# An encoder layer in fp32 on one core: Strassen steps in the down projections, a later attention step, a longer lag and earlier transposes

## The chip, the cores and the metric

The kernel runs on one core of a Trainium2 chip. The metric is device time in microseconds of that core. The times shown below are those of whole executions; the profile is of one further execution, with every instruction recorded. PE is TensorE, DVE is VectorE, ACT is ScalarE, POOL is GpSimd and SP is the queue that issues most loads.

## The reference

One layer over 256 tokens of width 2048, all in float32: a SwiGLU feed-forward block (FFN, inner width 5632) with half weight, two gated attention mixers side by side, and a second such FFN. Each part is framed by RMS norms.

```python
def swiglu(h, w_gate, w_up, w_down):
    return (jax.nn.silu(h @ w_gate) * (h @ w_up)) @ w_down

f = swiglu(rmsnorm(x, ffn1_pre_g), ffn1_w_gate, ffn1_w_up, ffn1_w_down)
x = x + 0.5 * rmsnorm(f, ffn1_post_g)
h = rmsnorm(x, mix_pre_g)
qa, ka, va, qb, kb, vb, ga, gb = jnp.split(h @ w_in, SPLITS, axis=-1)
...   # rope on q and k; sigmoid of ga, gb with a bias
out_a = windowed_gqa_sink(qa, ka, va, sink_logit)       # 8 heads on 2, |i-j| <= 128
out_b = differential_attention(qb, kb, vb, lam, ...)    # 4 heads, two softmaxes each
merged = ga * (out_a @ w_proj_a) + gb * (out_b @ w_proj_b)
x = x + rmsnorm(merged @ w_out, mix_post_g)
f = swiglu(rmsnorm(x, ffn2_pre_g), ffn2_w_gate, ffn2_w_up, ffn2_w_down)
x = x + 0.5 * rmsnorm(f, ffn2_post_g)
```

## The kernel before

**Products.** PE works in a rounded format, so every float32 operand is split in two: `hi`, a cast made by ACT (L178), and `lo`, the rest, a subtraction made by DVE (L180). A product of two operands is three matmuls: hi with hi, lo with hi, hi with lo (`mm3`, L201 to L203; `mm3s`, L259 to L261). The left operand (activations, transposed) is the stationary one, 128 x 128; 512 columns of a weight stream past it. Weights come from memory as units of 1 MB into `raw` (4 buffers), and are split into tiles `w` (6 buffers, so three pairs). `weights(k)` (L196) starts the split of unit k + `LA` (2) when unit k is used.

**Blocks.** `run_block` (L227) makes 512 columns of an output for both halves `h` of the tokens (2 x 128) and can let the second half lag by `lag` steps behind the first. `run_wide` (L263) makes 1024 columns: four results of 128 x 512, each in its own PSUM bank of eight. It walks over steps of 256 rows. A plain step ("N") is 24 matmuls. A step of kind "S" is one level of Strassen's method (seven products in place of eight, 21 matmuls): the weight unit gets three additions in place (L189 to L191) and a second pair of split tiles from the pool `big`; the left operand gets four sums and differences, made once by `make_forms` (L390, two steps share one `big` tile). The seven products have banks of their own, and after the last S step eight DVE operations and an ACT copy (L294 to L307) bring them together, after which plain steps go on in the same banks. `SKIND` gives the kinds of the eight steps of a gate or up block.

**An FFN** (`ffn`, L471) goes over eleven column blocks of the inner width in three parts, `PARTS`. Column block 0 is made alone, the others in pairs, first the gate block and then the up block of a pair. `up_after` multiplies, and defers the transposing of the result (`later`, L492) by a number of pumps; `pump` (L211) is called once a step. The transposed tiles `hT` (pool `big`, 9 tiles) are the left operand of the part's down blocks: two wide ones in parts one and two, whose results are added up in memory, and one wide and two narrow ones in part three, which end in the norm (`finish_f`) and the update of x (`post_norm`). All the down blocks' steps are plain.

**Seams.** Between FFN 1 and the mixer, and between the mixer and FFN 2, the last narrow block runs with `LAG`, and so does the first block after it. `make_xT` (L337) updates x (`upd`, L423), transposes it (L352) and writes the hi half on ACT (L358) and the lo half on DVE (L360) for each step of the first block. `tc.high_priority(HP)` moves what it holds ahead of 300 places in the order.

**Attention** runs between the steps of other blocks: `pipeline` (L816) is called by `pump` and at each tick runs the stages of several items, each stage at its own offset. `ItemB` has four stages: scores and softmax, transposing, product with v and norm (L738 to L740), transposing of the result (L750 to L754).

**What sets the order.** Only data dependences are written down. A planner (`schedule_with_timeline_sim=True`, L929) simulates the engines, gives out buffers and banks, and takes on each engine what is ready, by place in the program and priority. The order it finds is fixed in the program; on the chip every engine works through its own list.

Of the kernel before, what the change touches and what calls it, by code (L numbers as in the profile page):

```python
# [13 lines left out]
AF = mybir.ActivationFunctionType  # L14
ALU = mybir.AluOpType
# [10 lines left out]
NC = 512  # L26
# [3 lines left out]
NEG = -1e30  # L30
OFF_QA, OFF_KV, OFF_QB, OFF_KB, OFF_VB, OFF_GA, OFF_GB = 0, 1024, 1536, 2560, 3584, 4608, 6656
KU = D // (2 * P)
LAG = 2
LAG_END = 3
LA = 2
SKIND = "NSNSNSNN"
FIRST = (0, 2, 1, 4, 3, 6, 5, 7)
HP = 300
AHEAD = 2
# [5 lines left out]
def encoder_layer(  # L45
# [45 lines left out]
    def f32(ap):  # L91
        return ap.bitcast(F32)
# [50 lines left out]
    def queued(ins):  # L143
        return nullcontext() if ins is None else tc.issue_after(ins.ins)
# [63 lines left out]
    def later(fn, n=1):  # L208
        deferred.append([n, fn])
# [127 lines left out]
    def make_xT(gi):  # L337
        done = set()

        def pre(u, h):  # L340
            if (u, h) in done:
                return
            if not done:
                lo_of.clear()
            done.add((u, h))
            if h in upd:
                with queued(lo_of.get((u - AHEAD, h))):
                    upd[h](u)
            tp = tp_tile()
            for j in range(2):  # L350
                k = 2 * u + j
                nc.tensor.transpose(tp[:, j, :], x_sb[h][:, k * P:(k + 1) * P], ident)  # L352
            if h == 0:
                xT[u] = xTp.tile([P, 2, 2, SEQ], F32R, tag="xT", name=nm("xT"))
            t = xT[u][:, :, :, h * P:(h + 1) * P]
            gs = [gT[:, 16 * gi + 2 * u + j:16 * gi + 2 * u + j + 1] for j in range(2)]
            for j in range(2):
                hi_of[h] = nc.scalar.activation(t[:, 0, j, :], tp[:, j, :], AF.Copy, scale=gs[j])  # L358
            for j in range(2):
                lo_of[h] = nc.vector.scalar_tensor_tensor(  # L360
                    t[:, 1, j, :], tp[:, j, :], gs[j], f32(t[:, 0, j, :]), ALU.mult, ALU.subtract)
            lo_of[(u, h)] = lo_of[h]
            if u == 0:
                pre_ss[h] = small(4, f"pns{h}")
            if u % 2:
                n = u // 2

                def sq():
                    with queued(hi_of[h]):
                        nc.scalar.activation(t2(), x_sb[h][:, n * NC:(n + 1) * NC], AF.Square,  # L370
                                             accum_out=pre_ss[h][:, n:n + 1])
                if n == 3:
                    sq()
                else:
                    later(sq, 1)
            if u == KU - 1:
                s1 = small(1, "pn1")
                nc.vector.reduce_sum(s1, pre_ss[h], axis=AX.X)
                r_pre[h] = rsqrt_of(s1, 1.0 / D, EPS, "pn")
        return pre  # L380
# [6 lines left out]

    xS = {}

    def make_forms(kinds):  # L390

        for n, u in enumerate(u for u, k in enumerate(kinds) if k == "S"):
            if n % 2 == 0:
                fb = big([2, 2, 4, P])
            xf, sf = t2().rearrange("p (j t) -> p j t", j=2), t2().rearrange("p (f t) -> p f t", f=4)
            nc.vector.tensor_tensor(xf, f32(xT[u][:, 0]), f32(xT[u][:, 1]), ALU.add)
            a11, a12, a21, a22 = xf[:, 0, 0:P], xf[:, 1, 0:P], xf[:, 0, P:2 * P], xf[:, 1, P:2 * P]
            nc.vector.tensor_tensor(sf[:, 0], a21, a22, ALU.subtract)
            nc.vector.tensor_tensor(sf[:, 1], sf[:, 0], a11, ALU.subtract)
            nc.vector.tensor_tensor(sf[:, 2], a11, a21, ALU.subtract)  # L400
            nc.vector.tensor_tensor(sf[:, 3], sf[:, 1], a12, ALU.add)
            xS[u] = fb[:, n % 2]
            nc.scalar.copy(xS[u][:, 0], sf)
            nc.vector.tensor_tensor(xS[u][:, 1], sf, f32(xS[u][:, 0]), ALU.subtract)

    def split_T(src, n, hi, lo):
        tp = tp_tile()
# [63 lines left out]
    def ffn(post_g, pre, plan, lag, final, tail, x_src):  # L471
        hT = {}
        f = [None, None]
        ss = [small(4, f"fss{h}") for h in range(2)]
        last_c = [c_hi - 1 for _, c_hi in PARTS]

        def gate_up(c0, run_gate, run_up):
            s = {}

            def gate_after(h, c, acc):  # L480
                s[h, c] = t2()
                nc.scalar.activation(s[h, c], acc, AF.Silu, scale=r_pre[h])  # L482

            def up_after(h, c, acc):
                hh = t2()
                nc.vector.scalar_tensor_tensor(hh, acc, r_pre[h], s[h, c], ALU.mult, ALU.mult)

                def tr():
                    if c0 + c not in hT:
                        hT[c0 + c] = big([2, 4, SEQ])  # L490
                    split_T4(hh, hT[c0 + c], h)
                later(tr, 2 if c0 + 1 in last_c or c0 == 0 else len(SKIND))  # L492
            run_gate(gate_after)
            run_up(up_after)

        for part, (c_lo, c_hi) in enumerate(PARTS):
            for c in range(c_lo, c_hi):
                if c == 0:
                    gate_up(0, lambda a: run_block(plan["gate"][0], KU, lhs_x, a, lag, pre),
                            lambda a: run_block(plan["up"][0], KU, lhs_x, a))  # L500
                    make_forms(SKIND)
                elif c % 2:
                    gate_up(c, lambda a: run_wide(plan["gate"][c], lhs_x, xS.get, a),
                            lambda a: run_wide(plan["up"][c], lhs_x, xS.get, a))
            xlast = part == len(PARTS) - 1

            def down_after(h, c, acc, n, gb):
                if not xlast:
                    t = t2()
                    nc.scalar.copy(t, acc)  # L510
                    nc.gpsimd.dma_start(f_dram[h][:, (n + c) * NC:(n + c + 1) * NC], t,
                                        accum_op=ALU.add if part else ALU.bypass)
                else:
                    finish_f(acc, f, gb[c], ss[h], h, n + c, True, 4.0 / D, 4.0 * EPS, final)
            if xlast:
                for h in range(2):
                    f[h] = big([D], F32)
                    nc.gpsimd.dma_start(f[h], f_dram[h])
            lhs = lhs_of(hT, 2 * c_lo)
            for n in (0, 2):  # L520
                if xlast and n == 2:
                    reload_x(x_src)
                    for i in range(2):
                        gb = [load_bc(post_g[0, (n + i) * NC:(n + i + 1) * NC])]
                        run_block(plan["down"][part, n + i], 2 * (c_hi - c_lo), lhs,
                                  lambda h, c, acc, i=i, gb=gb: down_after(h, c, acc, 2 + i, gb),
                                  (LAG_END if final else LAG) if i else 0, tail=tail if i else None)
                else:
                    gb = [load_bc(post_g[0, i * NC:(i + 1) * NC]) for i in range(2)] if xlast else None
                    run_wide(plan["down"][part, n], lhs, None, lambda h, c, acc: down_after(h, c, acc, n, gb))  # L530

    def plan_ffn(w_gate, w_up, w_down):
        pl = {"gate": {}, "up": {}, "down": {}}
        for part, (c_lo, c_hi) in enumerate(PARTS):
            for c in range(c_lo, c_hi):
                if c == 0:
                    pl["gate"][0] = add_tall(w_gate[0], 0, D, 0)
                    pl["up"][0] = add_tall(w_up[0], 0, D, 0)
                elif c % 2:
                    pl["gate"][c] = add_wide(w_gate[0], 0, D, c * NC, SKIND, FIRST if c == 1 else None)  # L540
                    pl["up"][c] = add_wide(w_up[0], 0, D, c * NC, SKIND)
            r0, rows = c_lo * NC, (c_hi - c_lo) * NC
            pl["down"][part, 0] = add_wide(w_down[0], r0, rows, 0)
            if part < len(PARTS) - 1:
                pl["down"][part, 2] = add_wide(w_down[0], r0, rows, 2 * NC)
            else:
                for n in (2, 3):
                    pl["down"][part, n] = add_tall(w_down[0], r0, rows, n * NC)
        return pl
# [278 lines left out]
                  None if s else pres[1])  # L828
    run_wide(pm["qb"], lhs_x, None, q_after(qbT))
    run_wide(pm["vb"], lhs_x, None, v_after)  # L830
    ticker[0] = pipeline([ItemB(s, h, hh) for s in range(2) for h in range(2) for hh in range(2)], (0, 1, 2, 3), 1)
    run_block(pm["kv"], KU, lhs_x, kv_after)

    gates = {}
# [98 lines left out]
```

## Time and profile before

| | |
|---|---|
| three runs | 2080.92 us median (2079.74 to 2083.31) |
| the profiled execution | 2079.09 us, its span 2077.3 us |
| PE, weight loads of PE | 98% and 81% of the span, 9193 each |
| DVE, ACT, POOL | 69%, 48%, 3% |
| granted clock of TensorE, mean | 0.994 of full speed |
| DMA | 416 MB, 200 GB/s over the span |

Busy times are those of instructions on the engine; matmuls overlap their successors, so their mean duration is longer than the distance between two of them. "idle before <-" names what ended the wait of the instruction. A stretch of the second view below is named by its start.

### The profile page before, as it was taken

The numbers are of one execution on the slowest core, as the hardware profiler recorded it, in microseconds if no ns is written. First come the engines' busy times: TensorE is split into PE (matmuls) and PEld (weight loads), VectorE is DVE, ScalarE is ACT, GpSimd is POOL, SyncE is SP. The second block draws the span as 40 slices with busy tenths as digits, with TensorE's granted clock in tenths as the row PEclk, the third lists the DMA queues.
The fourth block names the chain that finished last, engine by engine and source line by source line (L and its number), as shares of the span: only waits on it lengthen the run. The fifth ranks groups of instructions, "written<-read, shape, count | busy, mean of one in ns | idle before, by whom it ended". The sixth has DMA issues, their size and how long they took to land. (4 is left out here: it accounts for less than half of the span.)

```text
span 2077.3 us, 22878 instructions
## 1 busy us (share of the span) xinstructions
PE 2036.5 (98%) x9193; PEld 1675.9 (81%) x9193; DVE 1431.5 (69%) x1413; ACT 987.9 (48%) x956; POOL 55.9 (3%) x91
## 2 busy tenths in 40 slices
PE   9999999999999999998999999999999999999997
PEld 7888887888878878887888888788888788887786
DVE  6984798647986675675675555569658885588854
ACT  7554545445554453454464344456445444454442
POOL 1000000000000010000000000000000000000000
PEclk9999999999999999999999999999999999999999
DMA  8556555676558646554545556546575656756672
GB/s 296 183 207 218 184 202 183 223 218 188 198 187 313 207 168 203 183 172 142 192 153 182 194 201 238 198 173 202 191 246 175 223 199 192 220 178 218 233 251 86
DMA packets 140570, 416.36 MB, mean 200 GB/s; under 512 B 8414, under 2 KB 9232, under 8 KB 139184
## 3 DMA queue, kind: packets, MB, share of 16 engines
q1 hardware_dynamic: 133872, 391.15, 54.7%
q0 software_dynamic: 6560, 23.75, 4.2%
q8 instruction: 72, 1.18, 0.2%
q14 instruction: 34, 0.28, 0.0%
q10 hardware_dynamic: 32, 0.01, 0.0%
HBM read 400.19 MB, written 14.68 MB: 200 GB/s over the span
## 5 line engine op out<-in xcount | busy, mean ns | idle before, releaser
L180 DVE TENSOR_TENSOR w<-raw,w 128x2048 fp32r<-128x2048 f32 (+3 forms) x376 | 796.5, 2123 | 492.5 <-ACT w L178 458.7
L178 ACT CAST w<-raw 128x2048 fp32r<-128x2048 f32 (+3 forms) x376 | 667.6, 1782 | 782.7 <-PE acc L260 607.7
L259 PE MATMUL acc<-w,xT 128*128 128x512 f32 x1368 | 536.0, 393 | 1.3 <-DVE acc L295 1.2
L260 PE MATMUL acc<-w,xT 128*128 128x512 f32 x1368 | 534.0, 390 | 0.0
L261 PE MATMUL acc<-w,xT 128*128 128x512 f32 x1368 | 513.0, 390 | 0.0
L259 PE MATMUL acc<-w,big 128*128 128x512 f32 x828 | 322.8, 390 | 1.1 <-ACT w L178 1.1
L260 PE MATMUL acc<-w,big 128*128 128x512 f32 x828 | 323.4, 391 | 0.0
L261 PE MATMUL acc<-w,big 128*128 128x512 f32 x828 | 318.0, 390 | 0.4 <-DVE w L180 0.4
L259 PEld LDWEIGHTS acc<-w,xT 128*128 128x128 f32 x1368 | 257.3, 188 | 57.6 <-DVE acc L295 3.0
L261 PEld LDWEIGHTS acc<-w,xT 128*128 128x128 f32 x1368 | 257.2, 188 | 53.3
L260 PEld LDWEIGHTS acc<-w,xT 128*128 128x128 f32 x1368 | 257.4, 188 | 51.7
L259 PEld LDWEIGHTS acc<-w,big 128*128 128x128 f32 x828 | 155.4, 188 | 34.0 <-ACT w L178 1.9
L261 PEld LDWEIGHTS acc<-w,big 128*128 128x128 f32 x828 | 155.5, 188 | 33.8 <-DVE w L180 2.0
L260 PEld LDWEIGHTS acc<-w,big 128*128 128x128 f32 x828 | 155.5, 188 | 31.7
L178 ACT CAST big<-raw 128x2048 fp32r<-128x2048 f32 (+1 forms) x64 | 118.9, 1860 | 89.2 <-DVE raw L191 85.4
L180 DVE TENSOR_TENSOR big<-raw,big 128x2048 fp32r<-128x2048 f32 (+1 forms) x64 | 141.5, 2219 | 23.0 <-ACT big L178 18.0
L202 PE MATMUL acc<-w,xT 128*128 128x512 f32 x208 | 82.5, 399 | 3.0 <-DVE xT L360 3.0
L201 PE MATMUL acc<-w,xT 128*128 128x512 f32 x208 | 82.0, 397 | 0.0
L203 PE MATMUL acc<-w,xT 128*128 128x512 f32 x208 | 79.3, 392 | 0.0
L201 PE MATMUL acc<-w,big 128*128 128x512 f32 x192 | 74.7, 389 | 0.0
L202 PE MATMUL acc<-w,big 128*128 128x512 f32 x192 | 74.7, 389 | 0.0
L203 PE MATMUL acc<-w,big 128*128 128x512 f32 x192 | 74.0, 389 | 0.0
(186 smaller groups left out, 1731.8 us busy)
## 6 DMA issues: line engine op xcount, KB each, us to landing
raw<-in_ffn_w_down SPq DMA_DIRECT2D x88, 1024.0 KB, 5.1
raw<-in_w_in SPq DMA_DIRECT2D x68, 1024.0 KB, 5.0
raw<-in_ffn_w_up SPq DMA_DIRECT2D x58, 1024.0 KB, 5.1
raw<-in_ffn_w_gate SPq DMA_DIRECT2D x57, 1024.0 KB, 5.2
raw<-in_ffn_w_gate SPq DMA_DIRECT2D x60, 512.0 KB, 4.7
raw<-in_ffn_w_up SPq DMA_DIRECT2D x60, 512.0 KB, 4.7
raw<-in_w_out SPq DMA_DIRECT2D x16, 1024.0 KB, 5.0
f_dram<-t POOLq DMA_DIRECT2D x32, 256.0 KB, 5.9
```

The source lines that it names most:

```text
L178: nc.scalar.copy(hi[:, sl], raw[:, sl])
L180: nc.vector.tensor_tensor(lo[:, sl], raw[:, sl], f32(hi[:, sl]), ALU.subtract)
L201: nc.tensor.matmul(o, lhi, rhi, start=first, stop=False)
L202: nc.tensor.matmul(o, llo, rhi, start=False, stop=False)
L203: nc.tensor.matmul(o, lhi, rlo, start=False, stop=last)
L259: nc.tensor.matmul(o, t[0], w[0][:, q, :], start=first, stop=False, skip_group_check=skip)
L260: nc.tensor.matmul(o, t[1], w[0][:, q, :], start=False, stop=False, skip_group_check=skip)
L261: nc.tensor.matmul(o, t[0], w[1][:, q, :], start=False, stop=last, skip_group_check=skip)
```

## The change

The down blocks of parts two and three that are made by `run_wide` get the kinds `DKIND`, with S at the second and the fourth of eight steps; the forms of their left operand are made after the gate block of the part's last pair, by a `make_forms` that takes any left operand. `LAG` goes from 2 to 3. The update of x and the two halves of x^T get priority. The transposes of an up block's first half of tokens are deferred by 2 pumps everywhere; those of the second half by 2 or 8 as before. The last stage of the differential attention's items runs one tick later.

```diff
-LAG = 2
+LAG = 3
 LAG_END = 3
 LA = 2
 SKIND = "NSNSNSNN"
+DKIND = "NSNSNNNN"
...
             if h in upd:
-                with queued(lo_of.get((u - AHEAD, h))):
+                with tc.high_priority(HP), queued(lo_of.get((u - AHEAD, h))):
                     upd[h](u)
...
-            for j in range(2):
-                hi_of[h] = nc.scalar.activation(t[:, 0, j, :], tp[:, j, :], AF.Copy, scale=gs[j])
-            for j in range(2):
-                lo_of[h] = nc.vector.scalar_tensor_tensor(
-                    t[:, 1, j, :], tp[:, j, :], gs[j], f32(t[:, 0, j, :]), ALU.mult, ALU.subtract)
+            with tc.high_priority(HP):
+                for j in range(2):
+                    hi_of[h] = nc.scalar.activation(t[:, 0, j, :], tp[:, j, :], AF.Copy, scale=gs[j])
+                for j in range(2):
+                    lo_of[h] = nc.vector.scalar_tensor_tensor(
+                        t[:, 1, j, :], tp[:, j, :], gs[j], f32(t[:, 0, j, :]), ALU.mult, ALU.subtract)
...
-    def make_forms(kinds):
+    def make_forms(kinds, lhs=None):
+        lhs = lhs or (lambda u: xT[u])
+        made = {}
...
+            v = lhs(u)
-            nc.vector.tensor_tensor(xf, f32(xT[u][:, 0]), f32(xT[u][:, 1]), ALU.add)
+            nc.vector.tensor_tensor(xf, f32(v[:, 0]), f32(v[:, 1]), ALU.add)
...
-            xS[u] = fb[:, n % 2]
-            nc.scalar.copy(xS[u][:, 0], sf)
-            nc.vector.tensor_tensor(xS[u][:, 1], sf, f32(xS[u][:, 0]), ALU.subtract)
+            m = made[u] = fb[:, n % 2]
+            nc.scalar.copy(m[:, 0], sf)
+            nc.vector.tensor_tensor(m[:, 1], sf, f32(m[:, 0]), ALU.subtract)
+        return made
...
-                later(tr, 2 if c0 + 1 in last_c or c0 == 0 else len(SKIND))
+                later(tr, 2 if h == 0 or c0 + 1 in last_c or c0 == 0 else len(SKIND))
...
         for part, (c_lo, c_hi) in enumerate(PARTS):
+            fS = {}
...
                 elif c % 2:
-                    gate_up(c, lambda a: run_wide(plan["gate"][c], lhs_x, xS.get, a),
-                            lambda a: run_wide(plan["up"][c], lhs_x, xS.get, a))
+                    off = 2 * c_lo
+                    def run_gate(a):
+                        run_wide(plan["gate"][c], lhs_x, xS.get, a)
+                        if c == c_hi - 2 and part:
+                            fS.update(make_forms(DKIND, lambda u: hT[(off + u) // 2][:, :, 2 * (u % 2):2 * (u % 2) + 2]))
+                    gate_up(c, run_gate, lambda a: run_wide(plan["up"][c], lhs_x, xS.get, a))
...
-                    run_wide(plan["down"][part, n], lhs, None, lambda h, c, acc: down_after(h, c, acc, n, gb))
+                    run_wide(plan["down"][part, n], lhs, fS.get, lambda h, c, acc: down_after(h, c, acc, n, gb))
...
-            pl["down"][part, 0] = add_wide(w_down[0], r0, rows, 0)
+            dk = DKIND if part else None
+            pl["down"][part, 0] = add_wide(w_down[0], r0, rows, 0, dk)
             if part < len(PARTS) - 1:
-                pl["down"][part, 2] = add_wide(w_down[0], r0, rows, 2 * NC)
+                pl["down"][part, 2] = add_wide(w_down[0], r0, rows, 2 * NC, dk)
...
-    ticker[0] = pipeline([ItemB(s, h, hh) for ...], (0, 1, 2, 3), 1)
+    ticker[0] = pipeline([ItemB(s, h, hh) for ...], (0, 1, 2, 4), 1)
```

## Rows read from the trace of the kernel before

**Rows 1.** The page, busy time, share of the span and instructions of each engine.
```profile
PE 2036.5 (98%) x9193; PEld 1675.9 (81%) x9193; DVE 1431.5 (69%) x1413; ACT 987.9 (48%) x956; POOL 55.9 (3%) x91
```

**Rows 2.** Stretches: length, each engine's busy time (instructions), clock, DMA share, GB/s.
```profile
293.90:340.00 46.10, 44.41 (x201) 35.84 (x200) 38.74 (x34) 23.37 (x19) 0.00 (x0) 1.00 0.54 183
340.00:381.80 41.80, 41.80 (x187) 34.61 (x186) 36.29 (x30) 21.41 (x15) 0.00 (x0) 1.00 0.58 201
381.80:426.90 45.10, 45.10 (x207) 37.34 (x206) 24.22 (x15) 20.55 (x16) 2.02 (x3) 1.00 0.57 190
426.90:470.40 43.50, 43.50 (x193) 36.02 (x192) 19.85 (x11) 17.12 (x12) 3.41 (x5) 1.00 0.74 219
470.40:512.70 42.30, 42.00 (x185) 34.23 (x185) 32.07 (x25) 20.38 (x15) 1.49 (x2) 1.00 0.75 219
...
710.20:735.70 25.50, 22.80 (x102) 18.26 (x100) 18.35 (x25) 11.92 (x16) 2.71 (x2) 1.00 0.69 236
735.70:766.10 30.40, 28.07 (x128) 22.14 (x129) 23.01 (x58) 17.99 (x50) 4.89 (x7) 0.94 0.41 144
...
903.30:965.00 61.70, 56.09 (x298) 48.01 (x297) 45.74 (x92) 35.50 (x78) 4.52 (x8) 0.97 0.45 149
965.00:1010.20 45.20, 45.20 (x195) 37.30 (x194) 18.37 (x13) 14.19 (x10) 0.00 (x0) 0.96 0.48 162
...
1315.50:1340.20 24.70, 22.44 (x102) 18.38 (x100) 15.24 (x21) 12.81 (x20) 0.64 (x2) 1.00 0.65 224
1340.20:1369.00 28.80, 27.64 (x125) 21.50 (x126) 20.26 (x51) 19.45 (x51) 3.25 (x6) 0.94 0.47 165
```

**Rows 3.** PE in order of time, near the start: start, us, operation.
```profile
17.75 1.47 PE L352 MATMUL tp<-ident,big 128*128 128x128 f32 x12
```

**Rows 4.** Waits of PE, whole span: total us, times, longest us.
```profile
PE tp L750 <- DVE t L740: 5.6, 1, 5.6
PE acc L259 <- ACT big L178: 3.5, 4, 0.9
...
PE acc L202 <- DVE xT L360: 3.0, 2, 2.1
PE tp L352 <- DVE big L423: 2.6, 1, 2.6
PE tp L409 <- ACT t L482: 2.6, 4, 0.7
PE acc L201 <- ACT xT L358: 2.3, 1, 2.3
```

**Rows 5.** DVE's groups by line and form: busy us, mean ns, idle before.
```profile
L180 DVE TENSOR_TENSOR w<-raw,w 128x2048 fp32r<-128x2048 f32 x290 | 663.4, 2288 | 413.3 <-ACT w L178 407.3 <-PE acc L260 5.2
L180 DVE TENSOR_TENSOR big<-raw,big 128x2048 fp32r<-128x2048 f32 x60 | 136.8, 2285 | 18.1 <-ACT big L178 18.0
L180 DVE TENSOR_TENSOR w<-raw,w 128x1536 fp32r<-128x1536 f32 x60 | 105.2, 1753 | 74.3 <-ACT w L178 46.6 <-issue 27.7
L189 DVE TENSOR_TENSOR raw<-raw 128x1024 f32<-128x1024 f32 x60 | 73.2, 1220 | 0.8
...
L190 DVE TENSOR_TENSOR raw<-raw 128x512 f32<-128x512 f32 x60 | 41.1, 686 | 0.5
...
L398 DVE TENSOR_TENSOR t<-t 128x128 f32<-128x128 f32 x6 | 1.7, 283 | 0.0
```

**Rows 6.** DVE in order of time, start of the up block.
```profile
342.52 1.76 DVE L180 TENSOR_TENSOR w<-raw,w 128x1536 fp32r<-128x1536 f32 x1 [6.92 <-issue]
```

**Rows 7.** DVE in order of time, end of the differential attention.
```profile
958.43 2.72 DVE L841 SCALAR_TENSOR_TENSOR t<-acc,pnr,t 128x512 f32<-128x512 f32 x4
961.07 2.28 DVE L180 TENSOR_TENSOR w<-raw,w 128x2048 fp32r<-128x2048 f32 x1
```

**Rows 8.** DVE in order of time, first block of the mixer.
```profile
758.86 2.28 DVE L180 TENSOR_TENSOR w<-raw,w 128x2048 fp32r<-128x2048 f32 x1
```

**Rows 9.** ACT in order of time, start of FFN 2.
```profile
1337.27 1.99 ACT L178 CAST w<-raw 128x1024 fp32r<-128x1024 f32 x2 [0.37 <-PE acc L202]
```

More of the change, by code (lines that the diff above doesn't have):

```diff
@@ L500, in ffn @@
                             lambda a: run_block(plan["up"][0], KU, lhs_x, a))
-                    make_forms(SKIND)
+                    xS.update(make_forms(SKIND))
                 elif c % 2:
-                    gate_up(c, lambda a: run_wide(plan["gate"][c], lhs_x, xS.get, a),
-                            lambda a: run_wide(plan["up"][c], lhs_x, xS.get, a))
+                    off = 2 * c_lo
[4 more added lines that the diff above has]
+                    gate_up(c, run_gate, lambda a: run_wide(plan["up"][c], lhs_x, xS.get, a))
             xlast = part == len(PARTS) - 1
@@ L830, in encoder_layer @@
     run_wide(pm["vb"], lhs_x, None, v_after)
-    ticker[0] = pipeline([ItemB(s, h, hh) for s in range(2) for h in range(2) for hh in range(2)], (0, 1, 2, 3), 1)
+    ticker[0] = pipeline([ItemB(s, h, hh) for s in range(2) for h in range(2) for hh in range(2)], (0, 1, 2, 4), 1)
     run_block(pm["kv"], KU, lhs_x, kv_after)
```

## The prediction

> **What bounds the kernel now.** I read the page's busy rows first, then the busy times by stretch, then TensorE's waits, then the instructions beside the largest waits.
>
> The busy row puts PE at 98% of a 2077.3 us span, DVE at 69%, ACT at 48% [rows 1]. The profiled execution took 2079.09 us, 1.8 us around the span; the median of the runs shown is 2080.92, so it lies 1.8 us under the median. A plain down block shows what PE does when nothing holds it: 192 products of 512 columns in 43.5 us (the two ends of the window add one record), 0.2266 us each (the stretch from 426.90) [rows 2]. The program has 8556 such products, 1939 us. The other 637 records of PE are transposes and short attention products; twelve transposes in a row take 1.47 [rows 3], 0.12 each, so these are 76 more. Some 62 us are not work: the start, the end and the waits below. Products that go away are therefore paid out nearly in full, and beside them only waits of PE can be won.
>
> The Trainium skill (Perfetto Trace Analysis, Identifying the Most-Contended Engine) says that matmul occupancy is a poor measure and that headroom is read from the busy share of LDWEIGHTS. By that the 81% here would mean a fifth to spare, and fewer products would bring little. The trace disagrees: in the down block at 426.90 PE waits for nothing and weight loads are still only 36.0 of 43.5 us, 83%. I keep the rule as a rival.
>
> PE's waits, with what each block took over its products (length less products times 0.2266, less 0.12 for each transpose):
> - last attention step: PE idle 5.6 us in one piece (L750) [rows 4], inside the block at 903.30; the clock is 0.97 there and 0.96 in the next block [rows 2]. At half clock (1.2 instead of 2.4 GHz) 0.04 x 45.2 = 1.8 us of the next block's work is lost.
> - end of FFN 1 and start of the mixer: 25.5 us for 96 products and 4 transposes, 3.3 over; 30.4 us for 96 and 32, 4.8 over (from 710.20 and 735.70) [rows 2]. In it 2.6 for L423, 2.1 (the longest of two) for L360 [rows 4], and the clock at 0.94, 0.06 x 30.4 = 1.8.
> - end of the mixer and start of FFN 2: 2.5 and 3.7 over (from 1315.50 and 1340.20) [rows 2]; 2.3 for L358, 0.9 (the rest of 3.0) for L360 [rows 4], the clock again 0.94, 1.7.
> - blocks such as 293.90, four times (gate of the second column pair of parts two and three): 46.1 - 41.5 - 16 x 0.12 = 2.7 each, where four deferred transposes fall at the gate block's end.
> - a wide S block after a plain down block (470.40, four times): 42.3 - 41.5 = 0.8. A wide up block (340.00) is 41.8 - 41.5 - 4 x 0.12, about 0.
>
> **The change, part by part.**
>
> *Strassen steps in six down blocks.* Two of eight row steps become 21 products instead of 24. Three wide blocks per FFN, two FFNs: 12 steps x 3 = 36 products fewer, 36 x 0.2266 = **-8.2 us**. All of them lie on PE, which sets the end.
>
> What it adds runs on DVE. A plain unit costs one 2.29 us subtraction; an S unit 1.75 + 1.22 + 2 x 0.69 + 2.29 = 6.64, so 4.35 more, 12 times 52 us [rows 5]. Closing a block adds eight operations of about 0.69, 5.5 us, six times 33. The forms of the left operand are per step 2 x 0.69 + 4 x 0.283 = 2.5, 5.0 per part, four times 20. Together 105 us on a DVE that has 646 idle: hidden as a sum, so the question is place.
> - Forms: DVE had 5.5 us free in the up block that takes them (36.3 of 41.8) and one hole of 6.9 just before its first weight split [rows 2, 6]. The last transposed halves of the previous pair are there by then, so I cost the forms at nothing. Without that cover they push up's splits back by up to 5.0 us, four times.
> - S phase: in a down block it is four steps, 90 products, 20.4 us, and the part's own transposes, 22.3 in the first block of a part. DVE must do two S units and two plain ones in it, 17.9; the first block also has 24.2 - 8 x 2.29 = 5.9 of evictions and transposes [rows 2, 5]. 23.8 against 22.3, less what starts early: nearly full. In the second block of a part 17.9 against 20.4 fits. No row shows an S phase in a down block. The bounds are 0 (340.00) and 2.7 (293.90) a block; I take 0.7, near the row that also follows a block boundary with a backlog (470.40): 6 x 0.7 = **+4.2**, ends 0 and +16.
> - Buffers: eight PSUM banks are full in that phase and the nine large buffers just suffice (four transposed tiles, two for x's forms or f, one for the new forms, one pair of weights), so the second S step's halves wait for the first step's products to let go. The plain step between (5.4 us) covers a 1.9 us cast and 2.29 subtraction. If not covered, it is in the 2.7.
> - Loads: the S units come as two halves instead of one, as the gate's already do, same bytes, DMA share 0.55 to 0.74 in these blocks [rows 2]. Nothing; a late one would add to the same stall.
>
> *Attention's last step one tick later.* Two transposes stand on PE for a chain (square, inverse root, scale) that sits on DVE behind four gate-bias operations, 2.72 us together, and a weight split of 2.28 [rows 7]. One tick is a plain step, 5.4 us of products that now stand ahead of the transposes. The wait goes to 0.2, and the lost clock with it: -(5.6 + 1.8) + 0.4 = **-7.0**. It moves two transposes, two ACT copies and two DVE subtractions, no DMA; their reader, the branch projection, comes after three more blocks. Late next is t2, a pool of eight: one more tile is alive (six of the item pipeline and two bias tiles). That is just eight; should it run over, a tick slips by about a step's wait, and 2 to 3 us come back. Ends: -7.4 and -3.
>
> *Lag 3 and priority at the two seams.* Lag 3 leaves six more products of the second half, 1.36 us, while the first half's norm runs. Priority puts the x update and the two halves of x^T ahead of weight splits. First seam: the 2.6 wait loses 1.36; the 2.1 wait goes, since a 2.28 split stood before L360 [rows 8]; of the 1.8 of clock I count half, as 1.2 of idle lies between the 0.9 that left the clock at 1.00 (293.90) and the 2.6 that did not. 1.4 + 2.1 + 0.9 = 4.4. Second seam: ACT ran a 1.99 us split pair ahead of L358 [rows 9]; with priority and 1.36 us of cover the 2.3 goes, with it the clock's 1.7 and the 0.9: 4.9. Sum **-9.3**. Cost: splits come later by the 0.6 to 1.1 us of what overtakes them, and with lag 3 three pairs of weights are alive of the six tiles, so in the tail block the fourth unit's split has one step, 2.7 us, for about 2.5. If it doesn't fit, 1 us a seam. The x writes on POOL's queue follow the update, not PE. Ends: -13 and -2.
>
> *Transposes of the first half after 2 pumps, not 8.* Eight of the 16 leave the end of four blocks where PE waited for L482 to free banks (2.6 in four) [rows 4], but their DVE and ACT work (1.3 us and 1.2) falls into the S phase of the gate block, whose last large cast was already 0.9 late [rows 4]. I take 0.75 off the 2.7: **-3.0**, ends -8 and +4.
>
> Sum: -8.2 + 4.2 - 7.0 - 9.3 - 3.0 = -23.3. Profiled 2079.1 - 23.3 = 2055.8; on the median 2080.9 - 23.3 = **2057.6 us**.
>
> **Rivals.**
> - *S phases fill DVE.* Each of the six costs the 2.7 of 293.90, not 0.7: +12.0, 2069.6. For: 23.8 against 22.3. Against: the second blocks fit. Chance 0.15.
> - *Everything moves well.* S phases cost nothing, both seams at their end, transposes gone: 2080.9 - 8.2 - 7.4 - 13 - 8, 2044. For: PE's order is re-planned around what is ready. Chance 0.07.
> - *The new plan keeps the waits.* The order comes from a simulated clock, which put the 5.6 us wait there in the first place; lag and priority only shift it. Strassen and half of attention remain: 2080.9 - 8.2 + 4.2 - 3.5 = 2073.4, up to 2080. Chance 0.10.
> - *The stream is not the bound.* The removed products turn into waits for splits (DVE 36.3 of 41.8 in up, 24.2 of 45.1 in down): 2057.6 + 8.2 = 2065.8. This is what the rule of the Trainium skill named above (Perfetto Trace Analysis) would give. The 43.5 us block without a wait speaks against. Chance 0.05.
> - *Slower: DVE bound at each part's last pair.* Forms land behind, not in, the 6.9 us hole: 4 x 5.0 = 20, the S phases that follow start late by as much and cost 2.7 each (16.2 instead of 4.2), and the seam's gains halve because splits are late there too: 2057.6 + 20 + 12.0 + 4.7 = 2094.3. It decides from the point where DVE has no hole over 1 us from the gate's end to the down block's fourth step. Chance 0.05.
>
> **How the numbers follow.** Forecast 0.58, its own range 2050 to 2066. The range for 8 in 10 takes in the full S phases and part of the plan that keeps its waits: 2046 to 2076. Within 0.2% (about 4 us, what a measurement of this kernel can tell) is 2076.8 to 2085.1. Faster: 0.57 + 0.14 + 0.07 + 0.04 + 0.05 = 0.87; same 0.07, mostly from the kept waits; slower 0.06.
>
> **What would show it.** 8520 products of 512 columns instead of 8556, at 0.2266. Down blocks with S of 186 products: right at 42.2 to 43 us without transposes, the S-phase rival at 45. The L750 wait gone and the clock at 1.00 through 1010. At the seams no wait for L360 over 0.5 us and at most one clock fall. The blocks like 293.90 at 45.3 us. The prediction is wrong if DVE has no hole before the up block's splits while PE waits for L178, L180 or L295 there, or if a wait of several us stands at a new place.

## The result, and the profile after

The changed kernel takes 2099.4 us (median of four runs, 2097.4 to 2101.35) beside 2081.43 for the kernel before on the same chip (2079.74 to 2083.31): a ratio of 1.0086, 95% interval 1.0073 to 1.0099. It is slower by 18 us where 23 less were forecast, and outside the range. The profiled execution took 2098.16 us, its span is 2096.4.

The busy row of the page after, to be read against [rows 1]: 36 fewer products, and PE, busy for about as long, fills less of a longer span. DVE has 144 more instructions and 96 us more work, where the prediction had counted 105.

```profile
PE 2034.7 (97%) x9157; PEld 1667.4 (80%) x9157; DVE 1527.3 (73%) x1557; ACT 1008.8 (48%) x982; POOL 55.8 (3%) x91
```

The same blocks by stretch, in the columns of [rows 2] (PE, PEld, DVE, ACT, POOL busy; clock; DMA share; GB/s):

```profile
295.70:341.00 45.30, 43.60 (x198) 35.58 (x197) 39.05 (x34) 22.79 (x19) 0.00 (x0) 1.00 0.53 186
341.00:385.80 44.80, 42.43 (x188) 34.49 (x187) 40.42 (x42) 22.45 (x17) 0.00 (x0) 1.00 0.54 188
385.80:433.40 47.60, 44.95 (x201) 35.88 (x200) 37.99 (x33) 22.07 (x17) 0.00 (x0) 1.00 0.46 159
433.40:477.20 43.80, 42.47 (x187) 34.76 (x186) 32.21 (x26) 21.77 (x18) 5.11 (x6) 1.00 0.76 231
...
720.80:745.60 24.80, 22.76 (x101) 18.21 (x99) 18.41 (x25) 11.87 (x16) 1.80 (x2) 0.99 0.77 263
745.60:777.20 31.60, 29.77 (x130) 23.23 (x130) 25.07 (x61) 18.15 (x50) 4.88 (x7) 0.90 0.37 134
914.30:970.00 55.70, 55.70 (x297) 47.40 (x295) 40.77 (x84) 29.93 (x67) 4.70 (x7) 1.00 0.47 159
970.00:1013.90 43.90, 43.90 (x198) 36.31 (x196) 23.30 (x22) 19.70 (x22) 0.55 (x1) 1.00 0.52 176
...
1343.90:1375.90 32.00, 27.89 (x125) 21.70 (x126) 20.75 (x51) 19.47 (x51) 3.25 (x6) 0.95 0.36 131
```

Beside [rows 2], with a removed product at 0.2266 us (six in a down block, 1.36):
- The up block that takes the forms: 44.8 for 41.8, +3.0. All four such blocks take 44.8; two of them had 43.2 before, so +9.2 for the four.
- The first down block of a part: 47.6 for 45.1 - 1.36, +3.9, four times: 15.5.
- The second: 43.8 for 43.5 - 1.36, +1.7, twice: 3.3.
- The last attention step and the block behind it: 55.7 for 61.7 and 43.9 for 45.2, the clock at 1.00 in both: -7.3.
- The first block of the mixer +1.2, with the clock at 0.90 for 0.94 (the last block of FFN 1 gives 0.7 back); the first of FFN 2 (1343.90) +3.2, with the clock at 0.95 for 0.94.

With -8.2 for the products, 2.3 in a gate block of FFN 2 behind a second down block, 1.3 at the start and -0.7 elsewhere this is 19.1, the difference of the two spans. The waits of PE after (total us, times, longest us):

```profile
PE acc L260 <- DVE acc L296: 14.1, 13, 1.4
PE acc L262 <- DVE big L181: 7.7, 8, 1.5
PE acc L260 <- ACT big L179: 6.0, 6, 2.3
PE acc L203 <- DVE xT L362: 4.3, 4, 1.8
...
PE acc L202 <- ACT xT L360: 3.9, 2, 2.3
PE acc L260 <- DVE acc L299: 3.8, 4, 0.9
```

(L179 and L181 are the cast and the subtraction of a split, before L178 and L180; L360 and L362 the halves of x^T, before L358 and L360; L296 to L308 the closing operations.) Beside [rows 4] the L750 wait is gone; the closings, L296 and L299, are the new head of the list. Of L296's 14.1, 8.0 lie in the six down blocks and 5.1 in the four gate blocks like 293.90, which waited for other things before. Three places show why.

**The up block.** DVE in order of time (start, us, operation, idle before and what ended it):

```profile
342.49 1.76 DVE L181 TENSOR_TENSOR w<-raw,w 128x1536 fp32r<-128x1536 f32 x1 [5.41 <-ACT w L179]
...
348.46 0.69 DVE L401 TENSOR_TENSOR t<-big 128x512 f32<-128x512 f32 x1
...
356.28 2.29 DVE L181 TENSOR_TENSOR big<-raw,big 128x2048 fp32r<-128x2048 f32 x1
...
369.30 0.70 DVE L409 TENSOR_TENSOR big<-t,big 128x512 fp32r<-128x512 f32 x1
```

and PE in the same block:

```profile
365.87 0.50 PE L260 MATMUL acc<-big,big 128*128 128x512 f32 x1 [0.90 <-ACT big L179]
...
369.45 0.96 PE L262 MATMUL acc<-big,big 128*128 128x512 f32 x3 [1.47 <-DVE big L181]
```

ACT at that time:

```profile
347.81 0.68 ACT L488 ACTIVATE t<-acc,pnr 128x512 f32<-128x512 f32 x1
```

The hole of [rows 6] is still there, 5.4 us, and empty. The forms (L401 to L409) come only after the last silu of the gate block (L488), from 348.46 on, between the splits of the Strassen units, which then reach PE 0.9 and 1.5 us late.

**The first down block.** DVE:

```profile
403.91 2.29 DVE L181 TENSOR_TENSOR w<-raw,w 128x2048 fp32r<-128x2048 f32 x1
406.12 0.69 DVE L296 TENSOR_TENSOR acc<-acc,t 128x512 f32<-128x512 f32 x1
406.72 2.28 DVE L181 TENSOR_TENSOR w<-raw,w 128x2048 fp32r<-128x2048 f32 x1
408.92 2.29 DVE L181 TENSOR_TENSOR big<-raw,big 128x2048 fp32r<-128x2048 f32 x1
411.12 2.29 DVE L181 TENSOR_TENSOR w<-raw,w 128x2048 fp32r<-128x2048 f32 x1
...
414.84 0.70 DVE L299 TENSOR_TENSOR acc<-acc,t 128x512 f32<-128x512 f32 x1
```

and what stopped PE:

```profile
406.87 0.50 PE L260 MATMUL acc<-w,big 128*128 128x512 f32 x1 [1.34 <-DVE acc L296]
413.46 0.50 PE L262 MATMUL acc<-w,big 128*128 128x512 f32 x1 [0.36 <-DVE w L181]
415.59 0.50 PE L260 MATMUL acc<-w,big 128*128 128x512 f32 x1 [0.94 <-DVE acc L299]
```

ACT in the same block:

```profile
404.26 1.91 ACT L179 CAST w<-raw 128x2048 fp32r<-128x2048 f32 x1
406.07 1.89 ACT L179 CAST big<-raw 128x2048 fp32r<-128x2048 f32 x1
```

DVE works from 386.9 to 418.0 with no gap over 0.3 us. At the first stop PE has made all products of the first four steps but twelve, those of the last Strassen unit's second pair (`big`). It waits for the first closing, L296, to go on with a later plain step; that closing stands behind the split of a later plain unit (403.91). The second pair is late in the same way: its cast (406.07) stands on ACT behind that of a later plain unit, its subtraction (408.92) on DVE behind two such splits. The twelve products therefore end only at 413, and then the next closings can run, up to the fourth (414.84), for which PE stops again. The three stops are 2.6 us of idle, and the restarts are slower. In the second down block PE stops once, 1.3 us, for an L296 that again stands behind one split; there DVE was idle for 2.1 us shortly before.

**The start of FFN 2.** ACT:

```profile
1340.97 1.99 ACT L179 CAST w<-raw 128x1024 fp32r<-128x1024 f32 x2 [1.80 <-PE acc L203]
...
1343.45 1.13 ACT L360 ACTIVATE xT<-tp,gT 128x128 fp32r<-128x128 f32 x4
...
1364.52 0.69 ACT L488 ACTIVATE t<-acc,pnr 128x512 f32<-128x512 f32 x1
...
1365.72 1.89 ACT L179 CAST w<-raw 128x2048 fp32r<-128x2048 f32 x1
1367.51 1.14 ACT L360 ACTIVATE xT<-tp,gT 128x128 fp32r<-128x128 f32 x4
```

The split pair of [rows 9] still stands ahead of the first hi half: the priority did not move it. With lag 3 the first half's silu (L488) and a split now also stand ahead of a later hi half, and PE waits once more.

### The profile page after: what moved, and what is told of

Same layout as the page of the kernel before. It is cut to its first block, busy times and chain, and to the rows that moved or that the text cites. A ratio compares the mean times of both kernels' runs of the same rounds, so it can differ in the third digit from the quotient of the medians.

```text
span 2096.4 us, 22995 instructions
## 1 busy us (share of the span) xinstructions
PE 2034.7 (97%) x9157; PEld 1667.4 (80%) x9157; DVE 1527.3 (73%) x1557; ACT 1008.8 (48%) x982; POOL 55.8 (3%) x91
## 5 line engine op out<-in xcount | busy, mean ns | idle before, releaser
L181 DVE TENSOR_TENSOR w<-raw,w 128x2048 fp32r<-128x2048 f32 (+3 forms) x376 | 789.4, 2108 | 417.0 <-ACT w L179 414.7
L179 ACT CAST w<-raw 128x2048 fp32r<-128x2048 f32 (+3 forms) x376 | 661.9, 1768 | 720.7 <-PE acc L261 564.5
L260 PE MATMUL acc<-w,big 128*128 128x512 f32 x768 | 300.5, 392 | 11.8 <-DVE acc L296 8.1
L261 PE MATMUL acc<-w,big 128*128 128x512 f32 x768 | 299.7, 390 | 0.0
L262 PE MATMUL acc<-w,big 128*128 128x512 f32 x768 | 290.6, 391 | 1.5 <-DVE w L181 1.5
L179 ACT CAST big<-raw 128x2048 fp32r<-128x2048 f32 (+1 forms) x76 | 141.6, 1865 | 99.3 <-DVE raw L192 95.3
L181 DVE TENSOR_TENSOR big<-raw,big 128x2048 fp32r<-128x2048 f32 (+1 forms) x76 | 169.1, 2232 | 25.8 <-ACT big L179 20.2
L260 PEld LDWEIGHTS acc<-w,big 128*128 128x128 f32 x768 | 144.2, 188 | 45.4 <-DVE acc L296 10.6
L262 PEld LDWEIGHTS acc<-w,big 128*128 128x128 f32 x768 | 143.9, 188 | 33.5 <-DVE w L181 3.9
L261 PEld LDWEIGHTS acc<-w,big 128*128 128x128 f32 x768 | 144.2, 188 | 29.3
L260 PE MATMUL acc<-big,big 128*128 128x512 f32 x228 | 89.7, 393 | 6.0 <-ACT big L179 6.0
L190 DVE TENSOR_TENSOR raw<-raw 128x1024 f32<-128x1024 f32 x72 | 88.1, 1223 | 1.4
L261 PE MATMUL acc<-big,big 128*128 128x512 f32 x228 | 88.9, 390 | 0.0
```

The source lines that it names most:

```text
L179: nc.scalar.copy(hi[:, sl], raw[:, sl])
L181: nc.vector.tensor_tensor(lo[:, sl], raw[:, sl], f32(hi[:, sl]), ALU.subtract)
L190: nc.vector.tensor_tensor(raw[:, 1::2], raw[:, 1:3], raw[:, 3:4].to_broadcast([P, 2, NC]), ALU.add)
L260: nc.tensor.matmul(o, t[0], w[0][:, q, :], start=first, stop=False, skip_group_check=skip)
L261: nc.tensor.matmul(o, t[1], w[0][:, q, :], start=False, stop=False, skip_group_check=skip)
L262: nc.tensor.matmul(o, t[0], w[1][:, q, :], start=False, stop=last, skip_group_check=skip)
```

## The experiments

The kernel before, with one part of the change each, comes first. Ratios are to the kernel before, timed beside each run on the same chip; its medians there are 2081.3 to 2082.6 us, so times of different runs compare to about 1 us.

**Attention alone.**

```diff
-(0, 1, 2, 3), 1)
+(0, 1, 2, 4), 1)
```

> The kernel before with the differential attention's last stage one tick later, nothing else. Theory A (the parts act where they stand, and the loss is in the Strassen steps and the seams): 7.3 us faster than before, 0.9965, PE's 5.6 us wait gone and no clock fall near 965. Theory B (the parts cost nothing alone; the planner's new order for all of them together makes the loss): also about 7 us faster, so this run checks the size only.

2073.39 us, ratio 0.9962 (0.9948 to 0.9977). The two blocks of [rows 2] at 903.30 and 965.00, the clock in the column after POOL's:

```profile
903.30:959.00 55.70, 55.70 (x296) 47.40 (x295) 40.90 (x84) 29.93 (x67) 4.71 (x7) 1.00 0.48 158
959.00:1003.00 44.00, 44.00 (x200) 36.45 (x199) 23.27 (x23) 19.98 (x21) 0.55 (x1) 1.00 0.53 179
```

The wait and its clock loss go with nothing in their place.

**Strassen with its forms alone** (the changed kernel with attention, transposes, lag and priority set back).

> The kernel before with the Strassen steps in the six down blocks and their forms, nothing else. Theory A: slower by about 20 us (8.2 less products; 9 more in the four up blocks that take the forms, 19 in the six down blocks), ratio 1.0096. Theory B: faster by some 4 to 8 us, since alone the S phases find the place they were given credit for.

2124.25 us, 1.0203 (1.0188 to 1.0218): 42 us slower, more than twice what the whole change loses: theory A in kind, at twice its size. By blocks: the down blocks lose what they lose in the changed kernel, but the four up blocks take 6.8 to 7.9 over their products instead of 2.9. So another part of the change softens the lateness of the forms there, most likely the early transposes; the runs don't separate it.

**The seams alone, then lag and priority apart.**

```diff
-LAG = 2
+LAG = 3
```

> The kernel before with lag 3 and the priority of the x update and of the halves of x^T, nothing else. Theory A: 3 to 5 us slower, with the wait for the first hi half still 2.4 us and a second wait of about 2 us late in FFN 2's first block. Theory B: faster by 5 to 9 us, as first forecast.

2086.7 us, 1.0026 (1.0015 to 1.0036), 4.7 slower: theory A.

> The kernel before with lag 3 alone. Theory L (the longer lag keeps a third pair of weights alive, the planner then plays the second half's products early, and the cover does not grow): the loss of the seams is the lag's, 4 to 6 us slower than before, ratio 1.002 to 1.003, the first wait for the hi half at FFN 2's start still 2.4 us. Theory H (priority is what hurts, by putting the splits behind): within 1 us of before.

2085.84 us, 1.0021 (1.0012 to 1.0031). The waits for x^T of the kernel with lag 3 alone:

```profile
PE acc L202 <- DVE xT L360: 3.9, 3, 1.8
PE acc L201 <- ACT xT L358: 3.9, 2, 2.3
```

Against [rows 4] (3.0 and 2.3) none got shorter by more than 0.3 and one more of each kind appeared; with the clock at 0.90 (0.94 before) the first block of FFN 2 is 4.5 longer. At the first seam the wait for L423 falls from 2.6 to 2.0.

> The kernel before with the priority of the x update and of the two halves of x^T alone. Theory L: the waits for L360 (2.1 and 0.9 us) go as forecast, 2 to 4 us faster. Theory H: 3 to 5 us slower.

2081.87 us, 1.0000 (0.9990 to 1.0010): neither theory. The planned order hardly differs from that of the kernel before: put side by side in order of time, 18 of 1413 DVE instructions and 12 of 956 on ACT are others than in the kernel before (by operation and tiles). The loss at the seams is the lag's.

**Transposes alone.**

```diff
-later(tr, 2 if c0 + 1 in last_c or c0 == 0 else len(SKIND))
+later(tr, 2 if h == 0 or c0 + 1 in last_c or c0 == 0 else len(SKIND))
```

> The kernel before with the transposes of the first half of tokens after 2 pumps everywhere, nothing else. Theory A: 1 to 3 us faster (the blocks of the second column pair lose 0.3 to 0.7 of their 2.7 each). Theory B: no change within 1 us.

2078.55 us, 0.9982 (0.9972 to 0.9991): 3.4 faster, a little more than theory A named. In the trace each pair of blocks like 293.90 and the up block ahead of it gains 0.4, the gate block from 46.1 to 45.3, the up block taking over four of its transposes: 1.7 for the four pairs. Another 0.6 and 1.0 are in the two last up blocks of part three.

**The changed kernel without its forms.** The Strassen steps of the down blocks use x's forms, which have the same size; the forms of their own left operand are left out.

> The changed kernel without making the forms of the down blocks' left operand; the S steps read x's forms instead, so the down products are of wrong operands while PE's work is the same. Theory F (the forms, 5 us of DVE, lie between the up block's weight splits): the four up blocks lose their 2.9 us of waits, 8 to 11 us faster than the changed kernel, about 2090. Theory G (the up blocks wait because large buffers or PSUM banks are short, not for DVE): no change within 2 us, 2098 to 2101.

2088.52 us, 1.0038 (1.0023 to 1.0053): 10.9 less than the changed kernel. The four up blocks fall by 3.0 each, to what [rows 2] shows at 340.00; the down blocks stay as they were (47.6, and 43.7 for 43.8). Of the 12 us, 3.4 come back in the gate and up block behind FFN 2's second down block. So the forms' lateness is the up blocks' loss, and not the down blocks'.

**The changed kernel without the three additions** on the Strassen units of the down blocks (their second operands are left as loaded).

> The changed kernel without the three additions on the weights of the down blocks' S units (2.6 us of DVE for each of 12 units; the second pair of tiles is then split from the plain weights, so the products are not the layer's). Theory C (the down blocks wait for the S unit's chain on DVE: split, additions, cast, split): the six down blocks lose 2.5 and 1.6 us, 11 to 15 us faster than the changed kernel, about 2086. Theory D (they wait for the closing operations, which stand behind weight splits however early the S unit is ready): 0 to 3 us faster.

2120.26 us, 1.0189 (1.0174 to 1.0204): both theories missed. With 12 x 2.6 = 31 us taken from DVE ([rows 5]; its busy time falls by 28.5) the kernel is 21 slower than the changed one. DVE in the first down block:

```profile
411.20 2.29 DVE L181 TENSOR_TENSOR big<-raw,big 128x2048 fp32r<-128x2048 f32 x1
417.23 0.69 DVE L298 TENSOR_TENSOR t<-acc,t 128x512 f32<-128x512 f32 x1 [3.75 <-PE acc L263]
```

DVE now has holes, and this block takes 11.3 over its products, 5 of them by a clock of 0.91; the other three first down blocks take 4.3 to 6.0 and the four up blocks 4.7 to 6.9. The planner found another order, with four transposes of each last pair moved into the down block. Only the second down blocks did as expected (1.7 to 0.3). The loss does not go by the amount of DVE work alone.

**Attention and transposes together.**

> The kernel before with the two parts that gained alone: attention's last stage a tick later, and the early transposes. If they add: 7.9 + 3.2 = 11 us faster than before, about 2071, ratio 0.9947. If the planner's new order for both undoes one: 2074 to 2078.

2071.03 us, 0.9942 (0.9925 to 0.9958): the two gains add up. This is the changed kernel's own gain with Strassen, lag and priority left out.

**Forms early.** The changed kernel with lag 2, without priority, and the forms made right behind the transposes that they need:

```diff
-                        if c == c_hi - 2 and part:
-                            fS.update(make_forms(DKIND, ...))
+                    if c == c_hi - 4 and part:
+                        later(lambda: fS.update(make_forms(DKIND, ...)), len(SKIND) - 1)
```

> The changed kernel with lag 2 and no priority, and with the forms asked for right behind the transposes they need, before the gate block's results take their buffers, so that DVE has them in its hole before the up block's splits. Theory F (the forms' place on DVE is what the up blocks pay for): the four up blocks lose 2.5 to 3 us each, the down blocks keep 4.1 and 1.7: 2099.4 - 4.5 for the lag - 11 = 2084. Theory M (it is the amount of DVE work around there, not the place): up blocks keep 2 us or more, about 2093.

2092.81 us, 1.0048 (1.0033 to 1.0063). The forms on DVE, first and last, and the up block:

```profile
333.86 0.68 DVE L401 TENSOR_TENSOR t<-big 128x512 f32<-128x512 f32 x1
...
340.03 1.29 DVE L409 TENSOR_TENSOR big<-t,big 128x512 fp32r<-128x512 f32 x2 [0.16 <-ACT big L408]
```

```profile
341.10:383.60 42.50, 42.16 (x188) 34.57 (x187) 37.16 (x31) 21.26 (x15) 0.00 (x0) 1.00 0.57 198
383.60:431.20 47.60, 44.92 (x201) 35.87 (x200) 37.99 (x33) 22.06 (x17) 0.00 (x0) 1.00 0.46 160
```

The hole can take them: 42.5 instead of 44.8, theory F by the blocks. The first down block keeps its 47.6, so its loss has another cause. The gain is not all kept, and so the time is the one that theory M named: the two gate blocks behind the second down blocks now take 3.0 and 4.2 over their products, 0.7 and 3.0 in the changed kernel, an up block behind them 2.3 more, and the seams give 3.2, not 4.5.

**Strassen steps third and sixth** instead of second and fourth, otherwise as the last one.

```diff
-add_wide(w_down[0], r0, rows, 0, dk)
+add_wide(w_down[0], r0, rows, 0, dk, (0, 2, 1, 4, 5, 3, 6, 7))
```

> As the run before, and the down blocks' two S steps stand third and sixth of eight with two plain steps between them, instead of second and fourth. Theory C (the S unit's chain on DVE, split, three additions, cast, split, and the plain unit's split behind it are late for PE since they start only when a weight pair comes free): the down blocks lose most of their 4.1 and 1.7 us, about 2084 - 15 = 2069, two us under attention and transposes alone. Theory D (the closing operations stand behind weight splits wherever the S steps are): the down blocks stay within 1 us of theirs, 2080 to 2086.

2088.77 us, 1.0027 (1.0018 to 1.0036). The second down blocks fall from 1.7 to 0.6 and 0.8, the first rise from 4.1 to between 5.8 and 6.9; but the granted clock is 0.93 in two of these and 0.97 in the other two, which is 3.5 and 1.5 us of their work, so without it they take 3.2 to 4.5. ACT there:

```profile
395.26 1.91 ACT L180 CAST w<-raw 128x2048 fp32r<-128x2048 f32 x1 [4.93 <-PE acc L262]
397.07 1.89 ACT L180 CAST big<-raw 128x2048 fp32r<-128x2048 f32 x1
```

The cast that PE waits for (2.2 us) stands behind one that itself waits 4.9 us for PE to free a pair of weight tiles. What made the first blocks dear was open still.

**Strassen steps fourth and sixth**, after three plain ones.

```diff
-add_wide(w_down[0], r0, rows, 0, dk, (0, 2, 1, 4, 5, 3, 6, 7))
+add_wide(w_down[0], r0, rows, 0, dk, (0, 2, 4, 1, 5, 3, 6, 7))
```

> As the kernel with the forms early (the changed kernel with LAG 2, no priority, forms behind the transposes), but the two Strassen steps of a down block are its fourth and sixth, after three plain steps (16 us). Theory B (the boundary: the first Strassen unit's splits meet the evictions and transposes that the up block leaves): the first down blocks fall from about 4 us over their products to 1.5 or less, four times, the second ones by 1 as with the third and sixth: 2092.8 - 10 - 2 = about 2081. Theory Q (the queue: a large cast stands on ACT behind a cast that waits for a free pair of weight tiles, wherever the Strassen step lies): the first down blocks keep 4 us or more and the time stays at 2089 to 2093.

2064.72 us (2061.85 to 2065.74), 0.9914 (0.9898 to 0.9931): theory B, and by more than it asked for. Its two down blocks of part two:

```profile
383.30:427.00 43.70, 43.70 (x201) 36.17 (x200) 35.10 (x30) 21.34 (x17) 1.15 (x2) 1.00 0.57 199
427.00:469.20 42.20, 42.20 (x187) 34.84 (x186) 31.60 (x24) 20.75 (x16) 3.47 (x5) 1.00 0.76 225
```

and DVE where the closing starts:

```profile
413.32 2.29 DVE L182 TENSOR_TENSOR w<-raw,w 128x2048 fp32r<-128x2048 f32 x1
415.53 0.69 DVE L297 TENSOR_TENSOR acc<-acc,t 128x512 f32<-128x512 f32 x1
```

PE is busy in all of both stretches. The first closing still follows a plain split, and so does the second pair's; but two more plain steps, 48 products or 10.9 us, now stand ahead of the last Strassen step. DVE has worked off what the boundary left (it is idle for 2.1 us before 408.78), and PE waits for nothing, if with little to spare: the closing at 415.53 ends as PE comes to need it. The two gate blocks behind take 2.2 and 3.5 less than with the forms early alone. This is faster than both kernels, and than attention with transposes alone by 6.3 (5.0 when each is set against the kernel before on its own chip, 6.0 by the traces), most of the 8.2 that the products are worth.

**Strassen in the second down block of part two alone** (third and sixth steps) on the kernel with attention and transposes.

> The kernel before with the attention step and the transposes moved, and Strassen steps (third and sixth) in the second down block of part two alone, two blocks in all, 12 products fewer (2.7 us), forms early. If the loss belongs to the first down blocks and to the forms behind the gate block: the two blocks take 0.5 to 0.9 over their products, the forms 0.5 each, so 2071.0 - 2.7 + 1.4 + 1.0 = 2070.7, no difference to the kernel without them. Rival (any Strassen step in a down block makes the planner's order worse around it): waits of 2 to 3 us in the gate and up blocks that follow, 2075 or more.

2073.39 us, 0.9961 (0.9946 to 0.9975), 2.4 above the kernel without them (3.7 when each is set against the kernel before on its own chip, 3.1 by the traces). Half of each theory: the two blocks take 0.3 over their products, the forms 0.65 each, but each of the two gate blocks behind takes 2.0 more.

**The order of the steps alone**, on the changed kernel with lag, priority and late forms left in.

> The changed kernel itself with one edit: the Strassen steps of the down blocks are the fourth and sixth instead of the second and fourth. LAG 3, the priority and the forms behind the gate block stay. Theory B (the boundary): the six down blocks lose their wait as before, 4 x 3.9 + 2 x 1.6 = 18.8, and nothing else moves: 2099.4 - 18.8 = 2080.6, level with the kernel before; the up blocks keep their 2.9. Rival G (the forms' lateness counts as well, because the forms are late only against a Strassen step that follows soon): the up blocks fall too, to 0.5, 9 us more, 2071. Rival K (it was the mixture with LAG 2 and the early forms that let the planner find the good order): 2090 or more.

2076.17 us (2075.26 to 2079.07), 0.9975 (0.9965 to 0.9984):

```profile
341.00:386.00 45.00, 42.63 (x190) 34.66 (x188) 40.42 (x42) 22.53 (x17) 0.00 (x0) 1.00 0.55 187
386.00:429.70 43.70, 43.70 (x201) 36.15 (x199) 35.10 (x30) 21.32 (x18) 1.17 (x2) 1.00 0.58 199
429.70:471.90 42.20, 42.20 (x187) 34.85 (x186) 31.60 (x24) 20.70 (x16) 3.44 (x5) 1.00 0.75 225
```

Theory B: the six down blocks lose their 18.7 us, and the up blocks keep their 3.0, so rivals G and K fall. The 2.5 in the gate block behind goes as well, and the first block of FFN 2 is 1.7 longer. By the traces this is 20.6 less than the changed kernel, by the medians 23.2.

## Why the prediction was wrong, step by step

- *What bounds the kernel*: right. In the down blocks of the order experiment (42.2 us for 186 products) a removed product pays its 0.2266 in full, and the rival that the stream is not the bound falls.
- *Strassen, -8.2*: right; 36 products fewer, all in blocks that can run without a wait.
- *S phases, +4.2*: the step that failed most. It compared DVE's work with PE's time over the whole phase (23.8 against 22.3), called that nearly full, and took 0.7 a block from a row whose closings come only after its sixth step. Measured are 3.9 in four and 1.7 in two, 18.8, a little beyond the upper end of 16. What the step left out is the due time and the place in the queue. It counted two plain units in the phase; in the trace DVE splits four before the second closing, and three of them (403.91, 406.72, 411.12) stand ahead of the second pair's subtraction or of closings that PE stops for. The 5.5 us of closings, counted in the 105, are missing from the 23.8. The order experiment removes all of the loss with the same work, so it is the place of the Strassen steps and not their work that costs. That the first blocks cost more than the second ones because of what the boundary leaves to DVE is supported by the row without gaps and by 3.9 against 1.7, but not shown alone: no run took the evictions and transposes away. The forms are not part of it (the first blocks lose the same without them), and the third and sixth steps lose as much by another queue, ACT's.
- *Forms, 0*: failed. The hole was real, but the forms were not in it: in the program they stand behind the gate block, and the first of them follows that block's last silu. The prediction asked whether the operands were there, not where the program puts the step; I take the temporaries, which gate results and forms share, to be what holds them, which is argued only. It named the price of that case rightly as a rival, 5.0 a block at most, and gave it 0.05; measured 3.0 in the blocks' rows, 10.9 in all by the run without forms.
- *Attention, -7.0*: right, -7.3 in the two blocks of the trace (8.6 alone by the medians); no slip from the tight pool.
- *Seams, -9.3*: failed in sign. The priority was counted as moving instructions that it did not move (no change alone). Lag 3 was counted as six products of cover; at FFN 2's start the first wait stayed 2.3 and a second pair of waits appeared: 4.5 lost at the second seam, 0.2 gained at the first (lag alone). In the changed kernel the first seam's waits did shrink, by 0.6 and 0.2, but the clock fell twice where it fell once before, and the first block of the mixer grew by 1.2.
- *Transposes, -3.0*: right in size, -3.4 alone, and the blocks like 293.90 take the 45.3 us named as the sign. But four transposes only moved to the up block ahead, so these pairs give 1.7; the rest comes from two up blocks that the prediction did not name. The agreement is in part luck.
- *The rival on the slower side* (2094.3) had the mechanism in most of its parts: forms behind the hole, S phases at more than 2.7. It was right in kind and had 5 of 100. That it lands 5 us from the measured time is in part luck: it let the late forms push the S phases back, and without the forms these lose the same; the hole that it thought gone was there.

With what the runs gave (products -8.2, S phases +18.8, forms +10.9, gate block +2.3, attention -7.3, seams +3.7, transposes -3.4, start +1.3) the sum is +18.1 where +18.0 was measured. Some of these terms are from medians and some from one trace, so the agreement is closer than they are certain.

The gate block behind a second down block is 2 to 3.4 us longer in some kernels and not in others, and the traces show by which choice of the planner. ACT in the changed kernel's one of FFN 2 (from 1815.1, 2.3 longer):

```profile
1841.65 1.91 ACT L179 CAST w<-raw 128x2048 fp32r<-128x2048 f32 x1 [6.72 <-PE acc L261]
1843.46 1.89 ACT L179 CAST big<-raw 128x2048 fp32r<-128x2048 f32 x1
```

As with the third and sixth steps, the large cast of the last Strassen unit stands behind one that waits for PE to free a pair of tiles, and PE then waits 2.3 us for it. In the same block of FFN 1 the large cast comes first (501.78 and 503.60), and nothing is lost. The runs with Strassen alone, without forms, without additions and with the forms early have the same wait of 2.2 or 2.3 in their longer blocks; with the second down block alone it is two others, 0.9 and 1.1. Why the planner takes one order here and the other there stays open.

## What to carry to other kernels

Work on an engine that is idle for a third of the time isn't hidden by that: write down when the bound engine needs each result and what stands ahead of it in its queue, above all where one block's end meets the next one's start. A step that adds work to such a queue should first be tried some plain steps further in: two steps' difference was worth 21 to 23 us here. The same holds for a large cast or split that PE needs soon: look for what stands ahead of it that itself waits for PE. And a hole in a profile can be used only by what the program's order and its buffers let in.

## What was not expected of the hardware and its plan

- Less work made the kernel slower (21 us with 28.5 us less for DVE), and a priority of 300 places changed nothing here: where a planner fixes the order, a change to one block alters it elsewhere, and only the trace of the new order tells what it costs.
- In the changed kernel's first down block waits of 1.3, 0.4 and 0.9 us within 10 us left the granted clock at 1.00; at the start of FFN 2, waits of 1.6 and 1.8 us within 4 us went with a clock of 0.95 over the block, 0.05 x 32 = 1.6 us of its work.
- After a wait the first product takes 0.50 us in the records instead of 0.39, and the next starts 0.11 later: a stop costs more than its idle time.
